# Sums of weights and of h in the seven-product pairs: additions on VectorE and in a DMA in place of GpSimd, h's sums from an fp32 copy, the pairs in the other order

## The chip, the core and the metric

The kernel runs on one core of a Trainium2 chip. The core has TensorE (PE: matmuls, with weight loads as PEld), VectorE (DVE), ScalarE (ACT), GpSimd (POOL) and SyncE (SP, which here only issues DMAs). Each engine works through its own queue in order; semaphores join them. The metric is the device time of one execution in microseconds, the median of several runs.

## What is computed

One layer of a hybrid encoder on 512 tokens of width 1024, all in float32:

```python
h = rmsnorm(x, norm_w)
proj = einsum('bsd,de->bse', h, w_in) + b_in       # 1024 x 11272
(mq, mk, mv, mi, mf, mo, mz, sq, sk, sv, sz, gates) = split(proj)
# A) mLSTM: causal conv and SiLU on mq, mk; 4 heads of 256; gates mi, mf
# B) stick-breaking attention: RMS-normed sq, sk; 8 heads of 128
merged = g_m * (y_m @ w_proj_m) + g_s * (y_s @ w_proj_s)
return x + merged @ w_out
```

## The kernel before

TensorE is used in a rounded fp32 form. Each fp32 operand is split into a high part (rounded, by ScalarE) and a low part (the rest, by VectorE), and a product is three matmuls: high by high, high by low, low by high. `hh` and `hl` are the parts of h, transposed; `wh` and `wl` those of a weight block.

The work is a list of units, each with one weight block of 512 KB (1024 columns in each of 128 partitions). Unit c's weights are split two units ahead, in three buffers. Python writes the program in the order of the units: at unit c it runs what `later[c]` holds (moved work, added by `defer`, `at` and `at_unit`), evacuates unit c-1, splits ahead, and writes unit c's matmuls in two halves, with pieces of attention heads between. The order of every engine's queue is therefore the order of this code, and the tables at the top (`SB_START`, `M_START`, `GATES_...`, in units, with E = 32) set where heads and gates go.

- Units 0 to 3: queries of the first four attention heads, token-major, while h is normalised and transposed. The small input gates `mi` and `mf` (`gates`, 16 matmuls with the weights `wg`) come before unit 3's matmuls.
- Units 4 to 17 and 18 to 31: two `Pair`s. A pair makes two column groups of 512 (c1, c2) for all tokens with seven half-size products in place of eight (Winograd's form): h is cut into 2 x 2 blocks (256 tokens by 512 rows of w_in), and so are the weights (raw tiles X, Z, Y, V). The products 1, 2, 6, 5, 7, 3, 4 take two units each. Products 6, 5, 7, 3 use sums of h (`form`, split into parts) and sums of weights made in place: t3 (Y), t2 (X), t4 (Z), t1 (X again). Results leave PSUM through copies `u` and tiles `dst`, which are loaded with the bias and to which GpSimd's DMAs add u. Pair 1 makes the keys and values of heads 0 to 3; pair 2 the values of heads 4 to 7 and of two mLSTM heads, which are parked in DRAM.
- From unit 32: channel-major groups, the rest of the projections, then the output projections. The heads are interleaved with them. `ty` and `tz` are queries or keys transposed by VectorE in blocks and put in place by 16 small DMAs each.

Of the kernel before, what the change touches and what calls it, by code (L numbers as in the profile page):

```python
# [37 lines left out]
def tile_hybrid_layer(  # L38
# [288 lines left out]

    def x_turn(tb):
        for g in range(2):
            x_tp(tb, g)  # L330
            x_hh(tb, g)
            x_hl(tb, *range(4 * g, 4 * g + 4))

# [10 lines left out]
    class SbSet:  # L344
# [19 lines left out]
        def qk_group(self, name, c0):  # L364
            row = []

            half = []

            def evac(tb, ps):
                if tb % 2 == 0:  # L370
                    half.extend(two("qk", name=name + "raw"))
                t = half[tb]
                nc.vector.tensor_tensor(t, ps, row[0], op=OP.add)  # L373
                if tb < 2 or name == "q" and self.s == 0:
                    self.norm(name, tb, t)
                else:
                    defer(1, lambda: self.norm(name, tb, t))

            tok_group(w_in, c0 + 512 * self.s, h_sta, evac, name == "q" and self.s == 0, c0 + 512 * self.s, row)

        def norm(self, name, tb, t):
            self.raw[name][tb] = t
            ssq = tiny.tile([128, 4], F32, name="ssq", bufs=2)
            rr = tiny.tile([128, 8], F32, name="r" + name, bufs=8 if name == "q" else 4)
            r = rr[:, 0:4]
            junk = blk("acc", BF, (128,), name="sqj")
            for h in range(4):
                nc.scalar.activation(junk, t[:, h * 128:(h + 1) * 128], AF.Square,
                                     accum_out=ssq[:, h:h + 1])
            rstd(r, ssq, 128, EPS)  # L390
            self.count[name] += 1
            last = self.count[name] == TB
            if name == "q":
                rn = rr[:, 4:8]
                nc.gpsimd.tensor_scalar(rn, r, -1.0, None, op0=OP.mult)
                self.r[tb] = (r, rn)
                if last:
                    by_plan(self.s, "q", lambda: self.turn(name, 0))
            else:
                def scale():  # L400
                    for h in range(4):
                        hs = slice(h * 128, (h + 1) * 128)
                        nc.vector.tensor_scalar(t[:, hs], t[:, hs], r[:, h:h + 1], None, op0=OP.mult)  # L403
                    if last:
                        done.add(("k", self.s))
                        by_plan(self.s, "k", lambda: self.turn(name, 1))
                defer(1, scale)

        def turn(self, name, g):
# [8 lines left out]
            def move():  # L418
# [3 lines left out]
                for b in range(4):  # L422
                    for a in range(4):
                        q = nc.gpsimd if self.s and a % 2 else nc.sync
                        q.dma_start(tz[32 * b:32 * b + 32, :, a, :], src[32 * a:32 * a + 32, b])
# [6 lines left out]
            if name == "q":  # L432
                defer(3, weight)
# [136 lines left out]
    gst = blk("y", shape=(KT, 8), name="gst")  # L570
# [306 lines left out]
    def h_part(t, row, col, i):  # L877
        k = 4 * col + 2 * i
        return t[:, k:k + 2, 256 * row:256 * row + 256].bitcast(F32)

    sums = {}

    def flat(tag, name):
        return blk(tag, shape=(516 if tag == "om" else 512,), name=name)[:, 0:512].rearrange("p (k t) -> p k t", k=2)

    def form_split(f, i, src):
        hi, lo = form[f][0][i], form[f][1][i]
        split(src, hi, lo)

    def form_sum(f, i):  # L890
        if i == 0 and f != 3:
            form_tiles(f)
        if f == 2:
            s1, t = flat("vl", "s1"), flat("acc", "st")
            nc.vector.tensor_tensor(s1, h_part(hh, 1, 0, i), h_part(hh, 1, 1, i), op=OP.add)
            nc.vector.tensor_tensor(t, h_part(hl, 1, 0, i), h_part(hl, 1, 1, i), op=OP.add)
            nc.vector.tensor_tensor(s1, s1, t, op=OP.add)
            s2 = flat("om", "s2")
            nc.vector.tensor_tensor(s2, s1, h_part(hh, 0, 0, i), op=OP.subtract)
            nc.vector.tensor_tensor(s2, s2, h_part(hl, 0, 0, i), op=OP.subtract)  # L900
            sums[1, i] = s1
            form_split(2, i, s2)
        elif f == 1:
            form_split(1, i, sums.pop((1, i)))
        elif f == 3:
            s3, t = flat("vl", "s3"), flat("tmp", "st")
            nc.gpsimd.tensor_tensor(s3, h_part(hh, 0, 0, i), h_part(hh, 1, 0, i), op=OP.subtract)
            nc.gpsimd.tensor_tensor(t, h_part(hl, 0, 0, i), h_part(hl, 1, 0, i), op=OP.subtract)
            nc.gpsimd.tensor_tensor(s3, s3, t, op=OP.add)
            sums[3, i] = s3  # L910
        else:
            s4 = flat("acc", "s4")
            hi, lo = form[2][0][i], form[2][1][i]
            nc.vector.tensor_tensor(s4, h_part(hh, 0, 1, i), hi.bitcast(F32), op=OP.subtract)
            nc.vector.tensor_tensor(s4, s4, lo.bitcast(F32), op=OP.subtract)
            nc.vector.tensor_tensor(s4, s4, h_part(hl, 0, 1, i), op=OP.add)
            form_split(4, i, s4)
# [13 lines left out]
    class Half:  # L931
# [9 lines left out]
        def split(self):  # L941
# [3 lines left out]
            split(self.pair.raw[name, self.g], self.wh, self.wl)  # L945
# [19 lines left out]
    class Pair:  # L965

        def __init__(self, c1, c2, got1, got2):
# [3 lines left out]
            self.sta = {1: h_form(0, 0), 2: h_form(0, 1), 6: s_form(2), 5: s_form(1),  # L971
                        7: s_form(3), 3: s_form(4), 4: h_form(1, 1)}
# [5 lines left out]
            for g in range(2):  # L978
                if first:
                    plan = {"X": g, "Z": g, "V": 1 + 2 * g, "Y": 2}  # L980
# [4 lines left out]
                self.at(b + g, self.t3, g)  # L985
                self.at(b + 1 + g, self.t2, g)
                self.at(b + 2 + g, self.t4, g)
                self.at(b + 4 + g, self.t1, g)
            for q, c in ((11, 0), (12, 3), (22, 4), (21, 6)):
                self.at(b + c, self.start, q)  # L990
# [20 lines left out]
        def t4(self, g):  # L1011
            z, x = self.raw["Z", g], self.raw["X", g]
            nc.gpsimd.tensor_tensor(z, z, x, op=OP.subtract)

        def t1(self, g):
            x, v = self.raw["X", g], self.raw["V", g]
            nc.vector.tensor_tensor(x, v, x, op=OP.subtract)

        def start(self, q):
            t = self.dst[q] = blk("qk", F32, (2, 512), name="dst")  # L1020
            nc.sync.dma_start(t, bass.AP(tensor=b_in.tensor, offset=b_in.offset + self.c[q % 10],
                                         ap=[[0, 128], [0, 2], [1, 512]]))

        def put(self, key, q):
            for tb in range(2):
                u = blk("tmp", name="u")
                nc.scalar.activation(u, self.bank[key, tb], AF.Copy)
                nc.gpsimd.dma_start(out=self.dst[q][:, tb, :], in_=u, accum_op=OP.add)

        def add(self, key, q):  # L1030
            for tb in range(2):
                t = self.dst[q][:, tb, :]
                nc.vector.tensor_tensor(t, self.bank[key, tb], t, op=OP.add)
                self.got[q % 10](2 * (q // 10 - 1) + tb, t)

        def evac(self, p):
            if p in (1, 6, 5):
                self.put({1: "a", 6: "a", 5: "b"}[p], {1: 11, 6: 12, 5: 22}[p])
            elif p in (2, 7):
                defer(1, lambda: self.add({2: "c", 7: "a"}[p], {2: 11, 7: 22}[p]))  # L1040
            else:
                self.add({3: "b", 4: "a"}[p], {3: 12, 4: 21}[p])

    def to_norm(s, name):
        return lambda tb, t: defer(1, lambda: sets[s].norm(name, tb, t))

    def to_parts(s):
        return lambda tb, t: defer(1 + tb % 2, lambda: sets[s].v_parts(tb, t))
# [3 lines left out]
    def to_dram(n):  # L1052
        return lambda tb, t: nc.sync.dma_start(v_park[n][128 * tb:128 * tb + 128, :], t)
# [12 lines left out]

    for i in range(2):
        at_unit(2 + i, form_sum, 2, i)
        at_unit(3 + i, form_sum, 3, i)
        at_unit(4 + i, form_sum, 1, i)  # L1070
        at_unit(6 + i, form_sum, 4, i)

    def s3_split(i):
        if i == 0:
            form_tiles(3)
        form_split(3, i, sums.pop((3, i)))
# [380 lines left out]
    later.setdefault(GATES_PREP, []).append(gates_prep)  # L1457
# [15 lines left out]
    for i in range(2):  # L1473
        at_unit(4 + i, s3_split, i)
# [23 lines left out]
    for c in range(N):  # L1498
# [15 lines left out]
        if c == 0:  # L1514
# [9 lines left out]
            gates_fill()  # L1524
# [47 lines left out]
```

## Time and profile before

| | |
|---|---|
| median of 3 runs | 756.45 us (755.95 to 756.66) |
| the profiled execution | 757.27 us, span 755.5 us, mean granted clock 0.963 |
| PE busy | 697.0 us (92%) |
| DVE busy | 524.5 us (69%) |
| ACT busy | 358.3 us (47%) |
| POOL busy | 157.7 us (21%) |
| DMA | 97.31 MB, mean 129 GB/s |

A row of the timeline gives start, length, engine, line, operation, output<-inputs with shapes, and in brackets the idle time before it with the engine and line that ended it. A matmul's length overlaps the next one's, so the step from start to start is its price. The PEclk column is the share of TensorE's full clock that was granted.

### The profile page before, as it was taken

To read this page: it belongs to the slowest core of one execution; us is meant where nothing else is said; L and a number is where in the kernel's file an instruction comes from. 1 tells how busy PE (TensorE), PEld (TensorE's weight loads), DVE (VectorE), ACT (ScalarE), POOL (GpSimd) and SP (SyncE) were. 2 spreads that over 40 slices of the span, in tenths; PEclk is the share of its full clock that TensorE was granted. 3 is DMA by queue.
4 is the path that set the end of the run, shared out by engine and by line. 5 is a ranking of instruction groups with operands and counts; after the bars stand their busy time and mean duration, and the time that the engine had idled before them with its cause. 6 is when DMAs were issued, how large, how long until landed. Compare 5 with 4: busy or idle time off the path is not lost.

```text
span 755.5 us, 9487 instructions
## 1 busy us (share of the span) xinstructions
PE 697.0 (92%) x3114; PEld 572.3 (76%) x3114; DVE 524.5 (69%) x863; ACT 358.3 (47%) x663; POOL 157.7 (21%) x292
## 2 busy tenths in 40 slices
PE   8585896966999999999979999999999999999998
PEld 6473574844887878888768888888888888888886
DVE  6868689643776789776879945559954436736797
ACT  5332553402547565466324477344474644434371
POOL 4267235100225545022000011100011110011010
PEclk9997898897899999999999999999999999999999
DMA  6523381626343365572454542433443234989523
GB/s 235 202 94 74 103 250 38 125 68 221 100 132 105 89 171 150 151 185 57 108 118 99 140 118 78 107 98 97 110 120 98 56 87 133 299 188 192 190 57 110
DMA packets 129040, 97.31 MB, mean 129 GB/s; under 512 B 19626, under 2 KB 106564, under 8 KB 128992
## 3 DMA queue, kind: packets, MB, share of 16 engines
q1 hardware_dynamic: 124624, 87.41, 40.5%
q0 software_dynamic: 4224, 9.18, 6.6%
q8 instruction: 24, 0.39, 0.2%
q14 instruction: 24, 0.20, 0.1%
q10 hardware_dynamic: 144, 0.13, 0.1%
HBM read 72.51 MB, written 5.30 MB: 103 GB/s over the span
## 4 chain that ended last, share of the span: by engine, by line
PE 57%; DVE 3%; SPq 2%; ACT 1%; issue 1%; DMA 1%; POOL 0%; DVEq 0%; ACTq 0%; POOLq 0%
PE dps L94 16%; PE dps L95 16%; PE dps L96 16%; PE aps L95 2%; PE aps L96 2%; PE aps L94 2%; SPq L641 1%; SPq L526 1%; PE aps L817 1%; PE aps L819 1%; PE aps L818 1%; DMA az<-ay 1%; DVE wl L100 0%; DVE kraw L403 0%; DVE atl L100 0%
## 5 line engine op out<-in xcount | busy, mean ns | idle before, releaser
L94 PE MATMUL dps<-hh,wh 128*128 128x512 f32 x448 | 177.7, 397 | 4.6 <-ACT wh L99 4.6
L95 PE MATMUL dps<-hl,wh 128*128 128x512 f32 x448 | 176.6, 394 | 0.0
L96 PE MATMUL dps<-hh,wl 128*128 128x512 f32 x448 | 176.5, 394 | 0.0
L100 DVE TENSOR_TENSOR wl<-stg,wh 128x1024 fp32r<-128x1024 f32 x76 | 92.8, 1221 | 81.2 <-ACT wh L99 81.1
L99 ACT ACTIVATE wh<-stg 128x1024 fp32r<-128x1024 f32 x76 | 80.0, 1053 | 66.4 <-DMA stg<-in_w_in_dram 34.3
L94 PEld LDWEIGHTS dps<-hh,wh 128*128 128x128 f32 x448 | 85.6, 191 | 21.8 <-ACT wh L99 5.0
L96 PEld LDWEIGHTS dps<-hh,wl 128*128 128x128 f32 x448 | 85.3, 190 | 19.1 <-DVE wl L100 1.0
L95 PEld LDWEIGHTS dps<-hl,wh 128*128 128x128 f32 x448 | 85.4, 191 | 17.0
L484 POOL TENSOR_SCALAR_AFFINE_SELECT om<-om 128x128 f32<-128x128 f32 x32 | 16.6, 518 | 131.0 <-ACT om L482 130.9
L94 PE MATMUL dps<-wh,hh 128*128 128x512 f32 x96 | 37.5, 391 | 0.9 <-DVE qraw L373 0.9
L96 PE MATMUL dps<-wh,hl 128*128 128x512 f32 x96 | 37.4, 390 | 0.0
L95 PE MATMUL dps<-wl,hh 128*128 128x512 f32 x96 | 37.4, 390 | 0.0
L708 DVE SCALAR_TENSOR_TENSOR acc<-tmp,vec,acc 128x511 f32<-128x511 f32 (+2 forms) x48 | 36.0, 750 | 1.7
L711 ACT ACTIVATE tmp<-acc 128x512 f32<-128x512 f32 x16 | 10.1, 634 | 52.0 <-DVE acc L708 52.0
L770 POOL TENSOR_SCALAR_AFFINE_SELECT w_all<-om 128x128 f32<-128x128 f32 x16 | 7.4, 495 | 123.8 <-DMA om<-rb_d 110.1
L958 PE MATMUL dps<-wh,form 128*128 128x512 f32 x64 | 24.4, 458 | 5.9 <-ACT wh L99 5.9
L490 DVE TENSOR_TENSOR_SCAN om<-om 128x512 f32<-128x512 f32 (+3 forms) x32 | 26.9, 840 | 3.3 <-POOL om L484 3.3
L482 ACT ACTIVATE om<-aps,rq 128x512 f32<-128x512 f32 (+3 forms) x32 | 16.7, 522 | 18.3 <-PE aps L96 18.3
L94 PE MATMUL dps<-yh,wh 128*128 128x512 f32 x64 | 24.9, 389 | 0.0
L95 PE MATMUL dps<-yl,wh 128*128 128x512 f32 x64 | 24.9, 389 | 0.0
L96 PE MATMUL dps<-yh,wl 128*128 128x512 f32 x64 | 24.9, 389 | 0.0
L958 PE MATMUL dps<-wl,form 128*128 128x512 f32 x32 | 15.1, 471 | 8.1 <-DVE wl L100 8.1
(309 smaller groups left out, 1588.6 us busy)
## 6 DMA issues: line engine op xcount, KB each, us to landing
stg<-in_w_in_dram SPq DMA_DIRECT2D x71, 512.0 KB
az<-ay SPq DMA_DIRECT2D x128, 40.0 KB
dst<-in_b_in_dram SPq DMA_DIRECT2D x8, 512.0 KB
stg<-in_w_proj_s_dram SPq DMA_DIRECT2D x8, 512.0 KB
B<-in_w_out_dram SPq DMA_DIRECT2D x8, 512.0 KB
stg<-in_w_proj_m_dram SPq DMA_DIRECT2D x8, 512.0 KB
wl<-stg POOLq DMA_DIRECT2D x8, 512.0 KB, 6.0
dst<-u POOLq DMA_DIRECT2D x12, 256.0 KB, 4.5
```

The lines of the kernel that those rows point to most:

```text
L94: nc.tensor.matmul(ps, ah, bh, start=first, stop=False)
L95: nc.tensor.matmul(ps, ah, bl, start=False, stop=False)
L96: nc.tensor.matmul(ps, al, bh, start=False, stop=last)
L99: nc.scalar.activation(hi, src, AF.Copy)
L100: nc.vector.tensor_tensor(lo, src, hi.bitcast(F32), op=OP.subtract)
L482: nc.scalar.activation(om[:, 0:n], zp, AF.Sigmoid, scale=rn[:, h:h + 1])
L484: nc.gpsimd.affine_select(out=om[:, ts], in_=om[:, ts], compare_op=OP.is_gt, fill=1.0, base=0, channel_multiplier=1, pattern=[[-1, 128]])
L490: nc.vector.tensor_tensor_scan(back, back, back, 1.0, op0=OP.mult, op1=OP.bypass)
L526: nc.sync.dma_start(az[32 * a:32 * a + 32, b, :, :], ay[32 * b:32 * b + 32, a, :, :])
L708: nc.vector.scalar_tensor_tensor(acc[:, j:], t[:, 0:T - j], cw(3 - j, ch), acc[:, j:], op0=OP.mult, op1=OP.add)
L711: nc.scalar.activation(t, acc, AF.Sigmoid)
L958: nc.tensor.matmul(pr.bank[key, tb], a, w[:, i, :], start=begin and n == 0, stop=end and n == 2, skip_group_check=again)
```

## The change

- h's sums: ScalarE also writes h in fp32 (`x_32`, tiles `h32`, 32 copies of 128 columns out of PSUM). VectorE forms the four sums in place from these, two 512-column subtractions or additions each, where before sums were made from the high and low parts, one of them on GpSimd. The new low part is one instruction with the sign in it.
- Weight sums: t3 is a DMA that adds a second block of `w_in` to Y; t4 goes from GpSimd to VectorE; t2 and t1 stay there. The signs are chosen so that all but t1 are additions.
- The low parts of product 1's weights in the first pair are made by ScalarE (a copy and a negated copy) and an adding DMA, without VectorE.
- Results: no bias is loaded into `dst`. VectorE adds a bias row to the PSUM bank, and a DMA then adds the copied other product u.
- The first pair now makes the parked values, the second the values and keys of heads 0 to 3.
- The gates move from unit 3 to unit 31, the squares of the first queries from units 0 to 3 to units 6 to 12, and half of the first set's `tz` transfers from SP's queue to GpSimd's. Some heads and the gates' scan start one or two units later.

TensorE, from the two small transposes of vectors ahead of unit 3 (before):

```order
L259 MATMUL aps<-ident,b_rows 128x56
L594 MATMUL aps<-hh,wg 128x512
L595 MATMUL aps<-hl,wg 128x512
L594 MATMUL aps<-hh,wg 128x512
L595 MATMUL aps<-hl,wg 128x512
```

The same place now, unit 3's first matmuls:

```order
L259 MATMUL aps<-ident,b_rows 128x56
L1446 MATMUL dps<-fh,hh 128x512
L1447 MATMUL dps<-fh,hl 128x512
L1448 MATMUL dps<-fl,hh 128x512
L1446 MATMUL dps<-fh,hh 128x512
```

The gates' matmuls (aps<-hh,wg) are gone from there; they stand ahead of unit 31's matmuls.

GpSimd in the first pair before (s and st are the third sum of h, rq the norm of the queries):

```order
L907 TENSOR_TENSOR s_452<-hh 128x512
L908 TENSOR_TENSOR st<-hl 128x512
L909 TENSOR_TENSOR s_452<-s_452,st 128x512
L282 TENSOR_SCALAR rq<-ssq 128x4
L283 TENSOR_TENSOR rq<-rq,mhalf 128x4
L395 TENSOR_SCALAR rq<-rq 128x4
L1005 TENSOR_TENSOR Y<-V,Y 128x1024
L907 TENSOR_TENSOR s_541<-hh 128x512
L908 TENSOR_TENSOR st<-hl 128x512
L909 TENSOR_TENSOR s_541<-s_541,st 128x512
L1005 TENSOR_TENSOR Y<-V,Y 128x1024
L1028 DMA dst<-u 128x512 x2
```

GpSimd now, from the end of the first pair to the second pair's end (wg is the gates' weight tile):

```order
L1036 DMA dst<-u 128x512 x2
L999 DMA Y<-in_w_in_dram 128x2x512
L1036 DMA dst<-u 128x512 x2
L999 DMA Y<-in_w_in_dram 128x2x512
L1036 DMA dst<-u 128x512 x2
L441 DMA tz<-ty 32x2x128 x16
L1036 DMA dst<-u 128x512 x2
L592 MEMSET wg 128x1024
L1036 DMA dst<-u 128x512 x2
```

Wide arithmetic has left GpSimd's queue; in its place stand DMAs that it issues, and the memset for the gates is behind them.

VectorE before, at products 6 and 5 of the first pair (s_604, s_631 are the fourth sum of h):

```order
L914 TENSOR_TENSOR s_604<-hh,form 128x512
L915 TENSOR_TENSOR s_604<-s_604,form 128x512
L916 TENSOR_TENSOR s_604<-s_604,hl 128x512
L100 TENSOR_TENSOR form<-s_604,form 128x512
L100 TENSOR_TENSOR wl<-X,wh 128x1024
L914 TENSOR_TENSOR s_631<-hh,form 128x512
L915 TENSOR_TENSOR s_631<-s_631,form 128x512
L916 TENSOR_TENSOR s_631<-s_631,hl 128x512
L100 TENSOR_TENSOR form<-s_631,form 128x512
L100 TENSOR_TENSOR wl<-X,wh 128x1024
L1017 TENSOR_TENSOR X<-V,X 128x1024
```

VectorE now, the same products (wl<-X of product 6, then of product 5; h_... are the sums in the fp32 tiles):

```order
L100 TENSOR_TENSOR wl<-X,wh 128x1024
L1008 TENSOR_TENSOR Z<-Z,X 128x1024
L906 SCALAR_TENSOR_TENSOR form<-h_340,form 128x512
L100 TENSOR_TENSOR wl<-X,wh 128x1024
L1033 TENSOR_TENSOR dst<-prow,aps 128x512 x2
L1012 TENSOR_TENSOR X<-X,V 128x1024
L1008 TENSOR_TENSOR Z<-Z,X 128x1024
L906 SCALAR_TENSOR_TENSOR form<-h_343,form 128x512
L897 TENSOR_TENSOR h_284<-h_278,h_284 128x512
L897 TENSOR_TENSOR h_287<-h_281,h_287 128x512
L100 TENSOR_TENSOR wl<-X,wh 128x1024
```

The three additions for each half of the fourth sum became one, and the two t4 (Z<-Z,X) now stand in VectorE's queue between the low parts.

The core of the diff:

```diff
-SB_START = [E + n for n in (0, 2, 5, 8, 14, 16, 20, 22)]
-M_START = [E + n for n in (36, 40, 54, 60)]
-GATES_PREP, GATES_START, GATES_SCAN = 2, 3, E + 22
+SB_START = [E + n for n in (1, 3, 6, 8, 14, 16, 20, 22)]
+M_START = [E + n for n in (37, 41, 54, 60)]
+GATES_PREP, GATES_START, GATES_SCAN = E - 3, E - 1, E + 24
...
-            later.setdefault(E + {"q": -7, "k": -3}[name], []).append(fn)
+            later.setdefault(E - 9, []).append(fn) if name == "q" else defer(2, fn)
...
+    def x_32(tb, g):
+        for k in range(4 * g, 4 * g + 4):
...
+            nc.scalar.activation(h32[at][:, k % 2, c:c + 128], x_ps[tb, g][:, k % 4 * 128:k % 4 * 128 + 128],
+                                 AF.Copy, scale=nw_t[:, k:k + 1])
...
-                        q = nc.gpsimd if self.s and a % 2 else nc.sync
+                        q = nc.gpsimd if a % 2 else nc.sync
...
-                defer(3, weight)
+                defer(3 if self.s else 6, weight)
...
+    def form_sum(f, i):
+        a11, a12, a21, a22 = h32[0, i], h32[0, 2 + i], h32[1, i], h32[1, 2 + i]
+        out, a, b, op = {5: (a22, a22, a21, OP.subtract), 7: (a21, a11, a21, OP.subtract),
+                         6: (a11, a22, a11, OP.add), 3: (a12, a11, a12, OP.subtract)}[f]
+        nc.vector.tensor_tensor(out, a, b, op=op)
...
+        nc.scalar.activation(hi, src, AF.Copy, scale=sign)
+        nc.vector.scalar_tensor_tensor(lo, src, sign, hi.bitcast(F32), op0=OP.mult, op1=OP.subtract)
...
+            if self.pair.base == 4 and self.p == 1:
+                nc.scalar.activation(self.wh, x, AF.Copy)
+                nc.scalar.activation(self.wl, x, AF.Copy, scale=-1.0)
+                nc.gpsimd.dma_start(out=self.wl, in_=x, accum_op=OP.add)
...
         def t3(self, g):
-            y, v = self.raw["Y", g], self.raw["V", g]
-            nc.gpsimd.tensor_tensor(y, v, y, op=OP.subtract)
+            r, c = 512 + 256 * g, self.c[2]
+            nc.gpsimd.dma_start(out=self.raw["Y", g], accum_op=OP.add,
+                                in_=w_in[r:r + 256, c:c + 512].rearrange("(k p) c -> p k c", p=128))
...
-            nc.gpsimd.tensor_tensor(z, z, x, op=OP.subtract)
+            nc.vector.tensor_tensor(z, z, x, op=OP.add)
...
+                nc.vector.tensor_tensor(t, self.row[q % 10], self.bank[key, tb],
+                                        op=OP.add if q % 10 == 1 else OP.subtract)
+                if q != 21:
+                    nc.gpsimd.dma_start(out=t, in_=u[tb], accum_op=OP.add)
...
-    Pair(C_SK, C_SV, to_norm(0, "k"), to_parts(0))
     Pair(C_SV + 512, C_MV, to_dram(0), to_dram(1))
+    Pair(C_SV, C_SK, to_parts(0), to_norm(0, "k"))
```

More of the change, by code (lines that the diff above doesn't have):

```diff
@@ L385, in norm @@
             r = rr[:, 0:4]
-            junk = blk("acc", BF, (128,), name="sqj")
+            junk = blk("om", BF, (128,), name="sqj")
             for h in range(4):
@@ L1523, in tile_hybrid_layer @@
             x_scale(3)
-            gates_fill()
+            for n in range(4):
+                x_32(n // 2, n % 2)
         if c == 1:
```

132 lines of the change are left out of this document (55 added, 77 removed).

## The prediction

> **What bounds the kernel now.** I count units as the code does: 0 to 3 are the first query group, 4 to 17 the first seven-product pair, 18 to 31 the second, 32 to 34 the next group. First view: busy time by stretch (microseconds long, then PE, PEld, DVE, ACT, POOL busy with instructions, clock, DMA share, GB/s).
>
> ```profile
> 30.00:172.00 142.00, 101.72 (x377) 78.16 (x377) 101.70 (x120) 53.36 (x109) 55.26 (x44) 0.86 0.40 106
> 172.00:198.30 26.30, 21.60 (x73) 16.60 (x74) 12.13 (x15) 10.11 (x15) 2.75 (x7) 0.76 0.57 173
> 198.30:380.00 181.70, 179.14 (x839) 149.07 (x838) 142.02 (x289) 99.60 (x213) 56.60 (x136) 1.00 0.47 123
> ```
>
> TensorE is the bound after 198 us. Before that it is short of input: in the 142 us from unit 3 to unit 32 it idles 40.3 us, and its clock is at 0.86. The waits of TensorE in the window from 29 to 172 us, with total, count and longest:
>
> ```profile
> PE dps L958 <- DVE wl L100: 9.1, 4, 6.9
> PE aps L594 <- DVE wg L584: 8.2, 1, 8.2
> PE dps L958 <- ACT wh L99: 5.9, 2, 4.7
> PE aps L958 <- DVE wl L100: 5.8, 5, 2.7
> PE dps L94 <- ACT wh L99: 4.6, 1, 4.6
> PE dps L958 <- DVE dst L1033: 4.5, 1, 4.5
> PE aps L958 <- ACT wh L99: 2.5, 1, 2.5
> ```
>
> They add up to 40.6 us, and all come from the chain that makes weights and sums. The timeline of TensorE gives the price of a matmul:
>
> ```profile
> 29.04 0.39 PE L1450 MATMUL dps<-fl,hh 128*128 128x512 f32 x1
> ...
> 37.95 0.77 PE L594 MATMUL aps<-hh,wg 128*128 128x512 f32 x1 [8.23 <-DVE wg L584]
> ...
> 41.07 0.52 PE L595 MATMUL aps<-hl,wg 128*128 128x512 f32 x1
> ...
> 48.74 0.39 PE L958 MATMUL dps<-wh,hh 128*128 128x512 f32 x1
> ...
> 53.95 0.39 PE L958 MATMUL dps<-wh,hl 128*128 128x512 f32 x1
> ...
> 63.91 0.50 PE L958 MATMUL aps<-wh,hh 128*128 128x512 f32 x1 [2.48 <-ACT wh L99]
> ...
> 66.90 0.63 PE L958 MATMUL aps<-wh,hl 128*128 128x512 f32 x1
> ...
> 70.74 0.63 PE L958 MATMUL aps<-wh,hl 128*128 128x512 f32 x1
> ...
> 171.97 0.80 PE L94 MATMUL dps<-hh,wh 128*128 128x512 f32 x1 [4.60 <-ACT wh L99]
> ...
> 187.55 0.50 PE L94 MATMUL aps<-ktt,qtt 128*128 128x512 f32 x1 [3.71 <-ACT ktt L99]
> ```
>
> 48.74 to 53.95 is 24 matmuls: 0.227 us a step at full clock. 66.90 to 70.74 is ten: 0.427 us at the low clock. Unit 3 (24 matmuls), the gates (16) and 28 units of 12 are 376 steps, 85.4 us at 0.227; they take 142.3 us from 29.7 to 171.97. So **56.9 us are lost**: 40.6 in waits, 16.3 in slow steps behind them.
>
> Why the chain is late, from the tile's instructions (min/median/max in ns) and from the timelines of VectorE and GpSimd:
>
> ```profile
> L1009 DVE TENSOR_TENSOR X<-X,Y x4: 1208/1760/4127, 57.1 to 120.9; 128x1024 f32<-128x1024 f32 x4
> ```
> ```profile
> 94.47 1.67 DVE L403 TENSOR_SCALAR dst<-dst,rk 128x128 f32<-128x128 f32 x8
> ...
> 122.00 7.73 DVE L403 TENSOR_SCALAR dst<-dst,rk 128x128 f32<-128x128 f32 x8
> ```
> ```profile
> 122.98 5.29 POOL L1013 TENSOR_TENSOR Z<-Z,X 128x1024 f32<-128x1024 f32 x2
> ```
>
> The same VectorE work takes 1.67 us alone and 7.73 beside GpSimd's subtraction; the 6.9 us wait follows it. An addition of 1.2 us has taken 4.1. A second cause is SP's queue, whose 32 small transposing transfers hold it for 22.6 us while a scale on VectorE and the loads behind them wait:
>
> ```profile
> 143.49 22.60 SPq L425 DMA_DIRECT2D tz<-ty  x32
> ```
>
> **The change, costed.** Prices on VectorE and ScalarE (start, length):
>
> ```profile
> 29.27 1.22 DVE L100 TENSOR_TENSOR wl<-X,wh 128x1024 fp32r<-128x1024 f32 x1
> ...
> 85.66 1.22 DVE L1017 TENSOR_TENSOR X<-V,X 128x1024 f32<-128x1024 f32 x1
> 86.79 1.28 DVE L1033 TENSOR_TENSOR dst<-aps,dst 128x512 f32<-128x512 f32 x2
> 88.09 1.23 DVE L100 TENSOR_TENSOR wl<-X,wh 128x1024 fp32r<-128x1024 f32 x1
> ```
> ```profile
> 15.60 0.19 ACT L300 ACTIVATION_READ_ACCUMULATOR junk<-x 128x1 f32 x1
> ...
> 63.88 1.08 ACT L1027 ACTIVATE u<-dps 128x512 f32<-128x512 f32 x2
> ...
> 88.91 0.31 ACT L388 ACTIVATE sqj<-dst 128x128 bf16<-128x128 f32 x1
> ...
> 92.26 1.99 ACT L99 ACTIVATE wh<-Y 128x1024 fp32r<-128x1024 f32 x2
> ...
> 191.54 0.37 ACT L482 ACTIVATE om<-aps,rq 128x128 f32<-128x128 f32 x1
> 191.81 0.36 ACT L486 ACTIVATE a_all<-aps,rq 128x128 f32<-128x128 f32 x1
> ```
>
> Start to start: VectorE 1.13 us for 1024 columns and 0.65 for 512; ScalarE 0.95 for 1024, 0.54 for 512, 0.27 for 128, and 3.35/8 = 0.42 for a square with its accumulator. Landing of a DMA that GpSimd issues, by group:
>
> ```profile
> L128 POOL DMA_DIRECT2D wl<-stg x8: 844/852/977, 661.3 to 699.4; - x8
> DMA to landing us min/median/max: 4.9/6.0/7.1
> ```
> ```profile
> L1028 POOL DMA_DIRECT2D dst<-u x12: 851/898/1201, 64.8 to 147.9; - x12
> DMA to landing us min/median/max: 3.3/4.5/7.3
> ```
> ```profile
> DMA to landing us min/median/max: 1.7/1.9/4.1
> ```
>
> The first adds 512 KB, the second 256 KB, the last (transfers of tile tz) 32 KB.
>
> Start of the changed kernel. ScalarE gets 32 copies of 128 columns out of PSUM (0.27 each, 8.6 us). It is free from 15.8 to 22, and the transposes that need the same banks come at 19.3 and 23; the first two blocks are copied by 18.0, so TensorE does not wait. The last block follows VectorE's last low part (end 29.3): 29.3 + 4 x 0.27 = 30.4.
>
> (a) Gates. Their 16 matmuls leave the start, and with them the 8.2 us wait: unit 3 runs from 29.7 to 35.1. They cost 16 x 0.227 = 3.6 us again before unit 31.
>
> (b) Unit 4. Both copies of X take 2 x 0.95: 32.3; GpSimd's adding DMA lands 6.0 later, 38.4. TensorE has been waiting since 35.3: 3.1 us (2.0 to 4.2 with landings of 4.9 to 7.1). The Trainium skill, "DMA: Bandwidth & Descriptors", section on the anatomy of one DMA, gives about 2.0 us plus bytes over 436 GB/s, for 512 KB an estimate of 3.2; by it the wait would be 0.3 and the sum 2.8 us lower. I take the row, which is this same adding transfer. Behind the wait come eight slow steps, as behind the 8.2 us gap (37.95 to 41.07): 8 x 0.2 = 1.6. The Trainium skill, "TensorE: Matmul & The Clock Gate", section on what is actually happening, asks for an idle window of about 3.4 us, by which 3.1 would leave the clock up and the sum 1.6 lower; the trace has slow steps from 66.90, behind a gap of 2.5 and a shorter one, so I keep them.
>
> (c) Units 5 to 17. VectorE's queue from 29.3 to the low part of unit 10's weights: 9 weight sums and low parts of 1024 columns (t2, t4, t1 and wl; two t4 are new there, from GpSimd) and one more wl: 10 x 1.13; 19 of 512 columns (3 query rows, 8 sums of h, 6 low parts, 2 results) x 0.65; 1.3 for the small vectors: 25.0. In-order waits: 0.5 for the last copy, 1.8 for the DMA sum Y (issued 35.3, lands 41.3), then ScalarE, which takes unit 5's bank (ready 45.2), a high part, four squares and the high part of X: about 3.7 more. So 60.3. TensorE reaches unit 10 at 35.1 + 4.7 + 6 x 2.72 = 56.1: wait 4.0, slow steps 1.6, and 0.5 at unit 12, where squares stand ahead of Y. Total of pair 1 with (b): 10.8; unit 17 ends at 35.1 + 38.1 + 10.8 = 84.0. GpSimd's 8 sums of h and 8 weight sums are gone, so no VectorE row is stretched.
>
> (d) Units 18 to 31. Half as much for VectorE, no sums of h. The DMA sums land some 10 us ahead of their use. I leave 1 us at units 24 and 25, where results, t1 and a low part fall between two units. With the gates: 84.0 + 38.1 + 3.6 + 1 = 126.7. Check by share: VectorE has 71 us of work in these 97 us, 73%; it had 101.7 of 142, 72%.
>
> (e) Unit 32. From the end of unit 27: two results 1.3, issue 0.9, landing 4.5 (at most 7.3), eight squares 3.4, high and low part 2.1: 12.2 (15.0), against 14.5 us that TensorE has left. Hidden, and just late at the longest landing. The 4.6 us wait there was for a load behind SP's 32 transfers; half go to GpSimd's queue and they issue two units earlier. So unit 32 starts at 126.7 instead of 171.97: **-45.3**.
>
> (f) 172 to 198. 72 steps are 16.3 us, the first head's scores and transposes about 2.4: 18.7 of 26.3. The 3.7 us wait at 187.55 was a late load too. The keys now come from the second pair, so their scale stands close before the first head: I leave 2.6 us. -5.0.
>
> (g) Later: TensorE is full, so nothing more is gained; each start of a head or of the scan moves by a unit or two, which I price at 0 between -3 and +4.
>
> Sum: -50.3, a walk with median durations in which two delays never meet. It keeps five or six waits where the trace had 15; I add 5 us, about half of what it keeps. So -45: of the profiled 757.27 (span 755.5, 1.77 around it) that is 712; the median shown, 756.45, is 0.8 lower: **711**. Its own range is 702 (no surcharge, shorter landings) to 719.
>
> **Rivals.**
> R1, adding DMAs in single file. If the four of 512 KB (two low parts, two Y) share the engines so that each lands 6.0 after the last, the second Y lands at 56.4 instead of 42. Its addition stands in VectorE's queue ahead of unit 8's low part: +9, with slow steps +12: 723. For it: the DMA share of that stretch is already 0.40. Against: the twelve result additions went in couples about 1 us apart and still landed in 4.5.
>
> R2, GpSimd's queue before the gates. Sixteen transposing transfers, two results, then the memset of the gate weights, whose casts stand on VectorE ahead of units 31 and 32. A stall there (the second row of VectorE's longest) costs up to 7.7, with the head's keys late behind it +10: 721.
>
> R3, slower. Chain every DMA that GpSimd issues until unit 31, each issued only after the last has landed: 6 x 6.0 + 12 x 4.5 + 16 x 1.9 = 120, from 32.4 to 152, still a gain. At the longest landings, 6 x 7.1 + 12 x 7.3 + 16 x 4.1 = 196, to 228: 56 later than unit 32 now, some 808. It turns at 140 us, 1.16 times the medians. Against it: the couples above. The Trainium skill, "SBUF — State Buffer", speaks for slow issue: GpSimd cannot write descriptors while VectorE runs a two-port operation. No row here shows an issue above 1.2 us.
>
> R4, the change does not do what it says: the stretched rows are only a symptom, and the chain on VectorE stays as slow. Then only the gate wait (8.2 and its slow steps) and the two load waits go, about 16: 740.
>
> **Chances.** Forecast 0.58; R1 0.15; R2 0.12; R4 0.08; R3 0.04; no change at all 0.03. The range 702 to 735 holds the forecast, R1 and R2, about 8 in 10 with the tails of each. A difference of 0.2% is about what a measurement can tell here: faster 0.93, same 0.03, slower 0.04.
>
> **What would show it.** (a) No wait on wg at 38 us. (b) A wait of about 3 us on a DMA at unit 4. (c) One of about 4 us on wl ten units into the stage; no VectorE row of 1024 columns above 1.3 us. (e) Unit 32 near 127 to 132. (f) 198.3's state reached near 150. I am wrong if the adding DMAs land far above 7 us, if VectorE waits at Y, or if TensorE waits later on than now.

## The result, and the profile after

The changed kernel takes 703.27 us (701.93 to 705.31), the kernel before 756.56 us in the same rounds: a ratio of 0.9298, 95% interval 0.9274 to 0.9323. The forecast was 711 with a range of 702 to 735. The profiled execution of the changed kernel, the slowest of its four, has a span of 703.6 us; the trace of before has 755.5.

First view, busy time by stretch as in the prediction: the old stretch of 142 us, and the same work now (unit 3 to unit 32, gates included).

```profile
30.00:172.00 142.00, 133.59 (x570) 107.94 (x571) 106.19 (x162) 78.80 (x158) 56.09 (x87) 0.96 0.63 157
30.00:130.45 100.45, 92.04 (x376) 73.19 (x377) 73.21 (x95) 55.02 (x111) 39.22 (x51) 0.95 0.70 168
```

In the first column behind the length stand TensorE's busy time and its matmuls: the work that took 142 us before takes 100 now (second row). TensorE's waits in the window from 29 to 172 us have shrunk from 40.6 us to 8.4 (total, count, longest):

```profile
PE aps L953 <- DVE wl L100: 3.7, 3, 2.4
PE dps L953 <- DMA wl<-X: 2.9, 1, 2.9
PE dps L953 <- DVE wl L100: 1.0, 2, 0.8
PE aps L953 <- ACT wh L99: 0.8, 2, 0.5
```

The timeline of TensorE at the steps of the prediction: start of unit 3, end of its work and the wait at unit 4, the last slow step, the wait at unit 10, the start of unit 18, the gates, unit 32, the first head's scores, and a wait that stands later.

```profile
29.86 0.50 PE L1446 MATMUL dps<-fh,hh 128*128 128x512 f32 x1
...
35.46 0.39 PE L953 MATMUL dps<-wh,hh 128*128 128x512 f32 x1
38.77 0.80 PE L953 MATMUL dps<-wl,hh 128*128 128x512 f32 x1 [2.93 <-DMA wl<-X]
...
44.49 0.51 PE L953 MATMUL dps<-wh,hl 128*128 128x512 f32 x1
...
58.46 0.50 PE L953 MATMUL aps<-wh,form 128*128 128x512 f32 x1 [0.49 <-ACT wh L99]
61.38 0.50 PE L953 MATMUL aps<-wl,form 128*128 128x512 f32 x1 [2.42 <-DVE wl L100]
...
85.20 0.39 PE L953 MATMUL dps<-wh,hh 128*128 128x512 f32 x1
...
124.10 0.39 PE L610 MATMUL aps<-hh,wg 128*128 128x512 f32 x1
...
130.45 0.39 PE L94 MATMUL dps<-hh,wh 128*128 128x512 f32 x1
...
144.54 0.39 PE L94 MATMUL aps<-ktt,qtt 128*128 128x512 f32 x1
...
210.78 0.76 PE L94 MATMUL dps<-hh,wh 128*128 128x512 f32 x1 [4.50 <-DVE kraw L387]
```

Neither the gates nor unit 32 waits for anything now. VectorE's additions and the landings of the DMAs that add (rows of the tiles X and Y, of product 1's wl, and of the results), as min/median/max:

```profile
L1004 DVE TENSOR_TENSOR X<-X,Y x4: 1220/1225/1226, 45.2 to 94.8; 128x1024 f32<-128x1024 f32 x4
```
```profile
L999 POOL DMA_DIRECT2D Y<-in_w_in_dram x2: 1531/1770/2009, 35.6 to 36.3; - x2
DMA to landing us min/median/max: 9.6/10.9/12.3
```
```profile
L938 POOL DMA_DIRECT2D wl<-X x2: 852/945/1038, 33.1 to 35.0; - x2
DMA to landing us min/median/max: 5.6/6.0/6.5
```
```profile
L1036 POOL DMA_DIRECT2D dst<-u x12: 849/1054/1252, 55.8 to 124.5; - x12
DMA to landing us min/median/max: 3.3/5.7/9.4
```

No addition X+Y is stretched any more (before: 1208/1760/4127). But the DMAs that add from DRAM to Y land after 9.6 to 12.3 us in the first pair, not after 6.0; VectorE's timeline shows what this did:

```profile
37.44 1.22 DVE L100 TENSOR_TENSOR wl<-Z,wh 128x1024 fp32r<-128x1024 f32 x1
45.25 1.23 DVE L1004 TENSOR_TENSOR X<-X,Y 128x1024 f32<-128x1024 f32 x1 [6.59 <-issue]
...
60.11 1.22 DVE L100 TENSOR_TENSOR wl<-X,wh 128x1024 fp32r<-128x1024 f32 x1
```

The trace does not show what ended the wait of 6.59 us ("issue"), but the issue of Y at 35.6 plus its landing after 9.6 is 45.2: VectorE stood for 6.6 us at Y. The last row is the low part of unit 10's weights, which TensorE then waits for.

From unit 32 on both traces hold the same 2112 matmuls of projections that write the tiles `dps`, so that the same matmul can be found in both by its number. The time by which the change is ahead there, and the length of each segment now and in two of the experiments below:

| from unit 32's matmul number | 0 | 72 | 288 | 504 | 720 | 792 | last |
|---|---|---|---|---|---|---|---|
| before, start (us) | 171.97 | 202.22 | 259.46 | 321.72 | 381.45 | 406.21 | 746.20 |
| after, start (us) | 130.45 | 148.66 | 210.78 | 274.60 | 333.56 | 351.86 | 693.97 |
| ahead by | 41.5 | 53.6 | 48.7 | 47.1 | 47.9 | 54.4 | 52.2 |
| segment after, from the number to the left | | 18.2 | 62.1 | 63.8 | 59.0 | 18.3 | 342.1 |
| the same, scan two units earlier | | 18.2 | 62.5 | 64.2 | 59.8 | 24.3 | 340.1 |
| the same, fourth head two units later | | 18.2 | 55.5 | 67.6 | 59.7 | 18.3 | 341.9 |

So 41.5 us come from the stretch that the prediction was about, 12.0 from the next 72 steps, and behind that the lead goes down by 6.5, up by 7.3 and down by 2.2.

### The profile page after: what moved, and what is told of

It reads as the page before. It is cut to its first block, busy times and chain, and to the rows that moved or that the text cites. A ratio compares the mean times of both kernels' runs of the same rounds, so it can differ in the third digit from the quotient of the medians.

```text
span 703.6 us, 9522 instructions
## 1 busy us (share of the span) xinstructions
PE 681.4 (97%) x3114; PEld 563.8 (80%) x3114; DVE 499.0 (71%) x857; ACT 367.7 (52%) x697; POOL 147.5 (21%) x308
## 4 chain that ended last, share of the span: by engine, by line
PE 64%; DVE 9%; issue 5%; DMA 4%; ACT 3%; SPq 2%; POOL 1%; DVEq 0%; POOLq 0%; ACTq 0%
PE dps L94 17%; PE dps L96 17%; PE dps L95 17%; PE aps L95 2%; PE aps L96 2%; PE aps L94 2%; DVE acc L724 2%; SPq L542 2%; DMA Y<-in_w_in_dram 2%; PE dps L953 2%; DVE wl L100 1%; DMA stg<-in_w_in_dram 1%; PE aps L953 1%; ACT sqj L404 1%; DVE tmp L730 1%
## 5 line engine op out<-in xcount | busy, mean ns | idle before, releaser
L500 POOL TENSOR_SCALAR_AFFINE_SELECT om<-om 128x128 f32<-128x128 f32 x32 | 14.1, 439 | 83.6 <-ACT om L498 83.6
L441 POOL DMA_DIRECT2D tz<-ty x48 | 25.9, 549 | 9.2 <-PE aps L953 5.0
L843 ACT ACTIVATE hns<-aps,hst 128x256 f32<-128x256 f32 x16 | 7.6, 475 | 29.8 <-DVE hst L842 22.6
```

The costliest lines, as they stand in the source:

```text
L500: nc.gpsimd.affine_select(out=om[:, ts], in_=om[:, ts], compare_op=OP.is_gt, fill=1.0, base=0, channel_multiplier=1, pattern=[[-1, 128]])
```

## The experiments

The kernel before took 753.1 to 754.9 us in the rounds of the experiments, and 756.6 in those of the result. So a difference of 2 or 3 us between kernels of different rounds is not shown by the times alone; where one is claimed below, the traces have to carry it. The ratios are to the kernel before in the same rounds.

The first four ask whether GpSimd's arithmetic beside VectorE was the cause, or only a symptom (R4).

**The kernel before without GpSimd's wide arithmetic.**

```diff
...
-            sums[3, i] = s3
+            sums[3, i] = h_part(hh, 0, 0, i)
...
-            nc.gpsimd.tensor_tensor(y, v, y, op=OP.subtract)
+            nc.gpsimd.tensor_tensor(y[:, :, 0:1], v[:, :, 0:1], y[:, :, 0:1], op=OP.subtract)
...
-            nc.gpsimd.tensor_tensor(z, z, x, op=OP.subtract)
+            nc.gpsimd.tensor_tensor(z[:, :, 0:1], z[:, :, 0:1], x[:, :, 0:1], op=OP.subtract)
```

> The kernel before, with GpSimd's wide arithmetic left out: t3 and t4 only touch one column in 512 of each slab (so products 6, 5, 7 and 4 get wrong weights), and the third sum of h is not formed (its first operand is split instead). VectorE's and ScalarE's work is as before, so only GpSimd's lateness and its effect on VectorE's rows go. Theory (GpSimd's wide operations stretched VectorE's rows and made the chain late): additions X+Y fall from 1.2 to 4.1 us to about 1.2, the scale of 7.73 us to about 1.7, and of the 23 us that TensorE waits for low and high parts between 29 and 172 us, with some 10 us of slow steps behind them, 20 to 33 go: 724 to 737 us. The gates' wait of 8.2 and the wait of 4.6 for a load behind SP's transfers stay. Rival (the stretched rows are a symptom, VectorE's own work sets the pace): under 8 us, 748 or more.

Measured: 730.77 us, ratio 0.9689 (0.9667 to 0.9712), so 24 us less. VectorE's additions, with the same instructions as before:

```profile
L1005 DVE TENSOR_TENSOR X<-X,Y x4: 1217/1218/1218, 54.6 to 106.3; 128x1024 f32<-128x1024 f32 x4
```

They are back at 1.2 us, as the theory wants; the rival's 748 is excluded. The stretch from unit 3 to unit 32 shows how much this is in sum:

```profile
30.00:149.72 119.72, 95.51 (x376) 74.27 (x377) 80.28 (x120) 52.61 (x109) 28.43 (x38) 0.92 0.47 126
```

VectorE's 120 instructions are busy for 80.3 us; in the kernel before its 120 of this stretch took 101.7. These 21.4 us are nearly the 22.3 by which unit 32 starts earlier (149.72 for 171.97). GpSimd's lateness by itself has little part in it: in the kernel before VectorE waited 1.4 us for a result of GpSimd, and its waits for ScalarE's high parts are no shorter here (27.1 us, before 26.1).

**The same arithmetic moved to VectorE**, in the kernel before:

```diff
...
-            nc.gpsimd.tensor_tensor(y, v, y, op=OP.subtract)
+            nc.vector.tensor_tensor(y, v, y, op=OP.subtract)
...
-            nc.gpsimd.tensor_tensor(z, z, x, op=OP.subtract)
+            nc.vector.tensor_tensor(z, z, x, op=OP.subtract)
```

> The kernel before, with t3, t4 and the third sum of h moved from GpSimd to VectorE as they stand, nothing else: eight instructions of 1024 columns and six of 512 more on VectorE, 8 x 1.13 + 6 x 0.65 = 12.9 us. Theory: VectorE's rows are no longer stretched, which is worth more than the added work: 735 to 748 us. Rival (symptom; VectorE's work sets the pace): 756 to 769 us. A third reading, that GpSimd's part was slow by itself and not the sharing: like the theory here, but the rows of VectorE beside GpSimd would not have been longer in the kernel before.

Measured: 740.99 us, ratio 0.9822 (0.9798 to 0.9846). VectorE has 12.9 us more to do, and the kernel is 13.9 us faster. TensorE's waits up to unit 32 are 30.0 us in place of 40.6; the kernel before did not need the DMA for this part of the gain.

**The changed kernel with t4 and h's sums back on GpSimd.**

```diff
-        nc.vector.tensor_tensor(out, a, b, op=op)
+        nc.gpsimd.tensor_tensor(out, a, b, op=op)
...
-            nc.vector.tensor_tensor(z, z, x, op=OP.add)
+            nc.gpsimd.tensor_tensor(z, z, x, op=OP.add)
```

> The changed kernel, with t4 (four additions of 1024 columns) and h's eight sums of 512 columns given back to GpSimd, same signs and same places; t3 stays a DMA. VectorE has 4 x 1.13 + 8 x 0.65 = 9.7 us less. Theory: GpSimd takes about 2.6 us for each wide addition and stretches what VectorE does beside it to two or three times; sums for products 6 and 5 come later, so units 8 to 12 wait: 709 to 722 us against 703. Rival (symptom): VectorE is relieved, 699 to 703 us.

Measured: 715.38 us, 12.1 more than the unchanged run beside it. GpSimd's and VectorE's timelines at the same places:

```profile
33.10 7.72 POOL L897 TENSOR_TENSOR h<-h,h 128x512 f32<-128x512 f32 x6
40.53 1.13 POOL L938 DMA_DIRECT2D wl<-X  x1
...
57.52 2.79 POOL L1008 TENSOR_TENSOR Z<-Z,X 128x1024 f32<-128x1024 f32 x1
...
63.52 3.02 POOL L1008 TENSOR_TENSOR Z<-Z,X 128x1024 f32<-128x1024 f32 x1
65.91 3.07 POOL L897 TENSOR_TENSOR h<-h,h 128x512 f32<-128x512 f32 x2
```
```profile
40.30 1.08 DVE L906 SCALAR_TENSOR_TENSOR form<-h,form 128x512 fp32r<-128x512 f32 x1 [10.19 <-ACT form L905]
...
57.97 3.41 DVE L100 TENSOR_TENSOR wl<-X,wh 128x1024 fp32r<-128x1024 f32 x1
...
63.64 5.89 DVE L906 SCALAR_TENSOR_TENSOR form<-h,form 128x512 fp32r<-128x512 f32 x1
69.46 1.21 DVE L100 TENSOR_TENSOR wl<-X,wh 128x1024 fp32r<-128x1024 f32 x1
```

The low part at 57.97 begins 0.45 us after GpSimd's addition and ends at 61.38, which is that addition's end (60.31) plus 1.1, the length of a low part alone. The row of 5.89 us begins 0.1 us after three additions of GpSimd in a row and ends 0.6 us after the last of them (68.98): VectorE is not slowed in these two rows, it stands until GpSimd is done. The Trainium skill, "SBUF — State Buffer", section on who interferes with whom, says just this: the port pair that the two share is taken as a lock for a whole instruction, by VectorE too when both inputs lie in SBUF. The trace agrees, in both rows.

But the two rows hold only 7.4 us more than the same instructions alone, and the 12.1 us have a second source, GpSimd's own lateness. Its first six sums of h take 7.72 us, where VectorE took 3.70; the second adding DMA of product 1 stands behind them in its queue and goes out at 40.53 in place of 35.03; and VectorE waits 10.2 us for parts made from these sums. This run does not separate the two.

**The changed kernel once more.**

> The changed kernel once more, unchanged, as the measure for the others on this chip and for what varies from run to run: 702 to 705 us by both theories. The wait of 4.5 us that TensorE has at 206 us for VectorE's evacuation of the second set's keys should stand in this profile too if it comes from the order of the queues, and be gone or of another size if it hangs on when a load lands.

Measured: 703.25 us (702.13 to 704.30). The wait for kraw is there again, 4.8 us in place of 4.5, which speaks for the order of the queues; the run with the fourth head moved, below, settles it.

The next three undo one step each.

**The gates back at unit 3.**

```diff
-GATES_PREP, GATES_START, GATES_SCAN = E - 3, E - 1, E + 24
+GATES_PREP, GATES_START, GATES_SCAN = 2, 3, E + 24
...
```

> The changed kernel with the gates back before unit 3's matmuls (and the second block of V loaded one unit later, since the gates' weights need its buffer). Theory (VectorE's chain up to unit 10 sets the pace of the first pair, so what TensorE does before it is free): the gates wait for their weights, which stand on VectorE behind six sums, to about 35, 5.5 us; unit 3 starts near 39 in place of 29.9; unit 4 then waits for nothing (2.9 and 2.8 of slow steps gone); unit 10 is reached at 60.6 and waits 1 to 2; behind unit 31 the 3.6 us of the gates are gone. Sum 0 to -3: 700 to 703 us. Rival (moving the gates is a gain of its own, as step (a) of the prediction counts it): the wait of 5 to 8 us with its slow steps comes back, 708 to 713 us.

Measured: 709.29 us, ratio 0.9397 (0.9379 to 0.9416), 6 us more: the rival, which is step (a), is right, and the theory I wrote here fell. VectorE's timeline there says why:

```profile
41.51 0.74 DVE L615 SCALAR_TENSOR_TENSOR g<-aps,gbias,g 36x512 f32<-36x512 f32 x1 [4.69 <-ACT g L613]
46.33 0.69 DVE L387 TENSOR_TENSOR qraw<-dps,brow 128x512 f32<-128x512 f32 x1 [4.07 <-PE dps L1448]
```

I had taken VectorE's chain for independent of TensorE up to unit 10. But unit 3's evacuation (qraw) stands in VectorE's queue ahead of the weight sums: a late unit 3 makes VectorE wait 4.1 us, and the gates' own evacuation 4.7.

By the traces that is the smaller part of the 6 us. Unit 18 starts at 89.83, against 84.2 to 85.2 in four traces with the gates at unit 31 (the changed kernel's two, and the runs with the scan and with the fourth head moved); but 3.6 us of this are the gates' work, which is then missing behind unit 31. TensorE ends unit 31 near 130.8 (127.9 to 130.4 in the four), and then waits:

```profile
133.10 0.50 PE L94 MATMUL dps<-hh,wh 128*128 128x512 f32 x1 [2.16 <-ACT wh L99]
```

With slow steps behind it the next 72 steps take 20.7 us in place of 18.2. ScalarE makes unit 32's high part behind squares of the second pair's results, which land late. So at unit 31 the gates also cover the time that unit 32's weights still need, a gain that step (a) did not name. (In the code it is the first block of V that is loaded one unit earlier, not the second one later; the second's load goes out only at 40.93.)

**All of the first queries' tz on SP's queue.**

```diff
-                        q = nc.gpsimd if a % 2 else nc.sync
+                        q = nc.gpsimd if self.s and a % 2 else nc.sync
```

> The changed kernel with all 32 transfers of the first queries' tz on SP's queue. Theory (SP's queue holds the loads of units 32 and on): they keep SP for some 22 us from 107 to 129, and the weights of unit 32 land near 132 to 134 and are split after that: TensorE waits 3 to 6 us at unit 32, 706 to 710 us. Rival (they issue two units earlier than before, and that is enough): 702 to 704 us.

Measured: 709.79 us, ratio 0.9407 (0.9390 to 0.9425), 6.5 us more. SP's queue, and TensorE at unit 32:

```profile
105.80 23.17 SPq L441 DMA_DIRECT2D tz<-ty  x32
129.07 2.09 SPq L119 DMA_DIRECT2D stg<-in_w_in_dram  x3
```
```profile
133.96 0.67 PE L94 MATMUL dps<-hh,wh 128*128 128x512 f32 x1 [4.68 <-ACT wh L99]
```

The load goes out at 129.07 only, and the wait of before (4.6 us) is back.

**The scan two units earlier.**

```diff
-GATES_PREP, GATES_START, GATES_SCAN = E - 3, E - 1, E + 24
+GATES_PREP, GATES_START, GATES_SCAN = E - 3, E - 1, E + 22
```

> The changed kernel with the gates' scan two units earlier, at E + 22 as before. Theory (before, the scan's loads of l_d and i_d held SP's queue for 8 us ahead of the block transfers az of a head, and TensorE waited 4.1 us for ath near 388 with slow steps behind it): the wait comes back near 335 to 340, 5 to 7 us, 708 to 710 us. Rival (the heads' own later starts took that wait away): 702 to 704 us.

Measured: 708.07 us, ratio 0.9384 (0.9366 to 0.9402), 4.8 us more. SP's queue, and TensorE:

```profile
324.12 6.23 SPq L657 DMA_DIRECT2D gfi<-l_d  x4
330.39 1.90 SPq L658 DMA_DIRECT2D gfi<-i_d  x1
332.33 4.95 SPq L542 DMA_DIRECT2D az<-ay  x8
```
```profile
339.43 0.51 PE L94 MATMUL aps<-ath,vh 128*128 128x512 f32 x1 [3.63 <-ACT ath L99]
```

The scan's five loads hold the queue for 8.1 us ahead of the head's block transfers. In the table above the segment from 720 to 792 is 24.3 us long, much as before (24.8), in place of 18.3.

The last five ask what is left at units 4 and 10 and at 206 us.

**t3 as an addition on VectorE.**

```diff
-            nc.gpsimd.dma_start(out=self.raw["Y", g], accum_op=OP.add,
-                                in_=w_in[r:r + 256, c:c + 512].rearrange("(k p) c -> p k c", p=128))
+            nc.vector.tensor_tensor(y, y, v, op=OP.add)
```

> The changed kernel with t3 as an addition of V on VectorE, in place of the DMA that adds a second block of w_in (2 MB less read in all): four more instructions of 1.13 us on VectorE, two of them in the first pair. Theory (the late landing of Y, 9.6 and 12.3 us after its issue, keeps VectorE idle from 38.7 to 45.2 and so sets unit 10): X+Y starts near 41, unit 10 waits 0 to 1 in place of 2.9, 699 to 702 us. Rival (VectorE's own amount of work sets unit 10): the two additions come on top, 705 to 708 us.

Measured: 700.77 us, ratio 0.9286 (0.9267 to 0.9305), 2.5 us less. X+Y starts at 39.77 in place of 45.25, though VectorE does more. TensorE still waits 2.42 us at unit 10, because both have moved: VectorE now waits 2.3 and 1.9 us for high parts, and the first of these starts on ScalarE at 42.76, just when TensorE's late unit 4 ends and would free its buffer (the trace does not show what ended ScalarE's wait).

So the first pair gains little: unit 18 starts at 83.57, against 84.2 to 85.2 in the four traces. Most of the gain is in the second pair, which I had not looked at. There TensorE now waits for nothing, where the four traces lose 1.8 to 3.5 us, and VectorE no longer stands at the second Y, as it did in the changed kernel:

```profile
94.82 1.23 DVE L1004 TENSOR_TENSOR X<-X,Y 128x1024 f32<-128x1024 f32 x1 [4.38 <-DMA Y<-in_w_in_dram]
```

Unit 32 starts at 125.32, against 127.9 to 130.5.

**Four instructions of h's sums behind unit 10's low part**, with t3 on VectorE:

```diff
-    for f, c in ((6, 3), (5, 5), (7, 7), (3, 9)):
+    for f, c in ((6, 3), (5, 5), (7, 9), (3, 11)):
...
-        at_unit(8, form_sum, 3, i)
+        at_unit(10, form_sum, 3, i)
```

> The changed kernel with t3 on VectorE, and with four of VectorE's 512-column instructions moved behind the low part that unit 10 waits for (the low parts of h's third sum two units later, the fourth sum two units later). Theory (with Y early, VectorE's queue up to unit 10's low part sets the wait there): that low part is done some 2.5 us earlier, 57 in place of 59.7, and the waits of 0.5 and 2.4 us at unit 10 with 1 to 2 us of slow steps go: 697 to 699 us. Rival (VectorE waits there for buffers that TensorE holds, not for its own queue): the wait stays, 700 to 702 us.

Measured: 698.83 us, ratio 0.9256 (0.9229 to 0.9284). The wait at unit 10 is 0.76 us and none at the next units is longer: the queue's own length set it. The 1.9 us against the run before would not be shown by the times alone; unit 32 starts at 123.04 in place of 125.32.

**Product 1's low parts on VectorE too.**

```diff
-            if self.pair.base == 4 and self.p == 1:
+            if False:
```

> As the kernel with t3 on VectorE and the four later instructions, and product 1's low parts in the first pair on VectorE too, so that no DMA adds weights any more: two more instructions of 1.13 us on VectorE ahead of unit 4. Theory (the adding DMA costs TensorE 3.1 us and 2.8 of slow steps at unit 4, and VectorE has waits of 2.3 and 1.9 us behind it to take in 2.3 us of work): unit 4 starts at 35.5 without a wait, unit 10 waits 2 to 4 again: 694 to 699 us. Rival (VectorE is the bound up to unit 10, so that what unit 4 gains is waited off there, and the two instructions come on top): 699 to 703 us.

Measured: 697.85 us, ratio 0.9251 (0.9228 to 0.9275), inside the forecast, but its time is not apart from the run before; unit 32 starts 1.0 us earlier, at 122.03. TensorE shows why it is so little: no wait at unit 4, and one of 3.1 us two units later.

```profile
43.62 0.79 PE L953 MATMUL aps<-wl,hh 128*128 128x512 f32 x1 [3.09 <-DVE wl L100]
```

**The fourth head two units later**, in the changed kernel:

```diff
-SB_START = [E + n for n in (1, 3, 6, 8, 14, 16, 20, 22)]
+SB_START = [E + n for n in (1, 3, 6, 10, 14, 16, 20, 22)]
```

> The changed kernel with the fourth attention head started at E + 10 in place of E + 8. Theory (TensorE's wait of 4.5 us for kraw near 206 us comes from the pieces of four heads that stand on VectorE ahead of that evacuation): some 6 us of the fourth head's scans, products and transposes leave the queue there, the wait goes with its slow steps, 696 to 700 us, unless the head's later parts meet another wait. Rival (VectorE stands there behind a transpose whose buffer a DMA still reads): the wait stays, 702 to 705 us.

Measured: 701.23 us, ratio 0.9295 (0.9272 to 0.9318). The wait of 4.5 us is gone, so the theory has the mechanism, but not the sum: the segment from 72 to 288 is 6.6 us shorter, and the next 3.8 longer, where the head's matmuls now stand and new waits with them. All segments of the table together are 2.3 us shorter. The new waits (window from 150 to 330 us):

```profile
PE aps L475 <- DVE kraw L419: 2.1, 2, 1.6
PE aps L95 <- DVE ktt L100: 1.9, 2, 1.0
```

**All of these together.**

> What the runs point to, in one kernel: no adding DMA for weights (t3 and product 1's low parts on VectorE), four 512-column instructions of h's sums moved behind unit 10's low part, and the fourth head started at E + 10. If the two gains stand beside each other, 697.9 less 2.0 (701.2 against 703.3 for the head alone): 695 to 697 us. If the earlier start of the stage only meets the same limits later, 698 us and no gain over the kernel without the head's move.

Measured: 695.10 us (694.89 to 695.97), ratio 0.9228 (0.9206 to 0.9250): 8.2 less than the changed kernel, with no DMA that adds weights in the pairs. The two gains stand beside each other: unit 32 starts at 122.10, as in the kernel without the head's move (122.03), and from there to the last matmul this one takes 1.5 us less.

## Why the prediction was right, and where its numbers were off

**What bound the kernel.** Shown from both sides: GpSimd's wide arithmetic is worth 24 us in the kernel before, and 12 for the part of it that was put back. In the kernel before nearly all of this is VectorE standing beside GpSimd, as the prediction had it; in the changed kernel GpSimd's own lateness has a part. Undone one at a time, that part, the gates (6.0), tz (6.5) and the scan (4.8) make 29 of the 53 us. The rest (t3 off GpSimd, fewer instructions for h's sums, results without a loaded bias, the pairs' order) was not separated, and whether the single parts simply add up was not tried.

**(a)** Unit 3 ran from 29.86 to 35.46 (forecast 29.7 to 35.1), and the gates moved back cost 6 us. The step had the wait for their weights right; but in that run more of the 6 us arise at unit 32, which the gates now cover.

**(b)** The landing of 5.6 to 6.5 us was the row's 6.0, and the wait 2.93 against 3.1. The slow steps were 14, from 38.77 to 44.49, 2.9 us in place of 1.6. The other price, the estimate of 3.2 us for 512 KB by the Trainium skill, "DMA: Bandwidth & Descriptors", section on the anatomy of one DMA, was too low by 2.4 and more.

**(c)** Right in sum, but by luck, since two errors cancel: the low part for unit 10 came at 61.3 (forecast 60.3), TensorE waited 0.5 and 2.4 us (4.0), and unit 17 ended at 85.2 (84.0). But Y landed at 45.2, not at 41.3, while of the 3.7 us that I had given to VectorE's other waits only 0.8 came. I had named three signs that I am wrong: that "the adding DMAs land far above 7 us", that "VectorE waits at Y", and that "TensorE waits later on than now". All three came (the third is the wait at 206 us, see (g)), and the time still fell, for the reason just given. Rival R1 was half right: the second Y landed at 48.6, between my 42 and its 56.4, and t3 on VectorE gains 2.5 us in all, not 12. Whether the source in DRAM or the crowd (DMA share 0.70) makes these landings long stays open.

**(d), (e)** Pair 2 lost 3.5 us (85.20 to 130.45 is 45.2; 38.1 and the gates' 3.6 are work) where I left 1; the three other traces with the same pairs lost 1.8 to 2.8. "The DMA sums land some 10 us ahead of their use" was wrong: the second Y of this pair went out at 81.59, landed 13.1 us later, and VectorE stood 4.38 us for it (2.65 to 3.74 in the others). With t3 on VectorE the pair loses nothing. Unit 32 started without a wait, at 130.45 against 126.7: -41.5, not -45.3.

**(f)** This term was mis-sized: -12.0 for -5.0. I cut the stage at 198.3 us, but its 72 steps end at 202.22 in the trace of before, and I left 2.6 us for a late k scale that didn't come. The old stage is 30.25 us for 18.5 of work (16.3 and 2.2 of the heads); 4.7 of the rest are waits, and most of what is left are slow steps (clock 0.76 in the prediction's second row). The new one has no wait and the full clock: 18.21 us for 17.8.

**(g)** Priced at 0 and measured +1.3, but of parts that I had not seen: the fourth head's pieces crowd VectorE ahead of an evacuation (6.5 us lost with slow steps, of which the head's later start gave back 2.0), and the later scan frees SP's queue for a head (6.5 gained in that segment; the scan moved back cost 4.8). "TensorE is full, so nothing more is gained" was wrong: the wait on ath near 389 had a queue behind it that the change moves.

**The sum.** The terms made -50.3; the traces have -52.2 at the table's last matmul: +3.8 at unit 32, -7.0 in (f), +1.3 in (g). That the two are so near is partly luck, since the errors have different signs. The surcharge of 5 us for delays that meet is about what the first stages and (g) lost beyond their terms (5.1), though whether by delays that met is not shown. So the term that failed is (f), priced at -5.0 and measured at -12.0: its 7.0 us are most of the 7.7 by which the forecast of 711 was too high. R2 did not occur (the memset at 118.2 is done before the gates start at 124.1, though VectorE waited 1.4 us for it), nor did R3; R4 is excluded by the first two experiments.

## What to carry to other kernels

Where rows of the same VectorE instruction differ by two or three times, look at what GpSimd does at that moment, and count its time as VectorE's: moving the work to VectorE itself can be faster than running it beside. A transfer that adds from DRAM is no free addition: price it by its landing in the stage where it will run, and keep an addition on VectorE when VectorE would wait for it. When a table of starts moves, look at each in-order queue for what it now stands ahead of, also where TensorE is full.

## What the runs showed of the hardware that I had not expected

A wait near 3 us may or may not cost TensorE's clock, and the slow steps can begin late. Behind waits of 2.60 and 3.00 us (the run with the scan moved, and the last kernel) the next two dozen steps were at full speed; behind 2.75, 2.78, 2.93, 3.09, 3.11 and 3.12 us in six others seven to fourteen steps took 0.43 us in place of 0.23. With four instructions moved, the wait at unit 4 was 2.75, and the first three steps behind it were not yet slow:

```profile
38.27 0.50 PE L953 MATMUL dps<-wl,hh 128*128 128x512 f32 x1 [2.75 <-DMA wl<-X]
38.61 0.40 PE L953 MATMUL dps<-wh,hl 128*128 128x512 f32 x1
38.84 0.39 PE L953 MATMUL dps<-wh,hh 128*128 128x512 f32 x1
39.07 0.54 PE L953 MATMUL dps<-wl,hh 128*128 128x512 f32 x1
39.41 0.63 PE L953 MATMUL dps<-wh,hl 128*128 128x512 f32 x1
```

The Trainium skill, "TensorE: Matmul & The Clock Gate", section on what is actually happening, gives a free-running window of about 3.4 us, and the low clock after an idle one. That the outcome hangs on the moment and not on the length alone agrees with these rows; that a wait needs 3.4 us to cost the clock does not. Nor is a shorter wait safe: one of 2.42 us at unit 10, with one of 0.5 to 0.7 just ahead of it, was followed by slow steps in each of seven runs. Behind the single waits the price is nothing or 1.7 to 2.9 us, not much less than the runs of the changed kernel differ (3.4).
